# Last super-block: the new key and value rows of three head pairs by block transposes and a DRAM way, the last two projection jobs over 512 columns, and the last row tile scaled on two engines

## The chip, the cores and the metric

One core of one Trainium2 chip. The metric is device time in microseconds (us) of one execution. The kernel before takes 1251.13 us, the median of three runs (1250.59 to 1251.42). The engines are called as in the profile: PE is TensorE (matrix products and PE transposes), PEld its weight loads, DVE is VectorE, ACT is ScalarE, POOL is GpSimd, and SP is the engine that issues nearly all DMAs.

## The reference

One layer of a streaming encoder on 2048 prompt rows and 64 sample rows of width 1024. RMSNorm, one input projection into 4096 features, two head groups side by side, an output projection, a residual and a last RMSNorm:

```python
aq, ak, av, ag, hq, hf, hi, hg = split(rms_norm(x, ln_g) @ w_in)      # 8 x 512 features
o_a = attention(aq, ak, av, rel_bias) * silu(ag)                      # 8 heads x 64, band of 576 keys
o_b, S = hgrn2(hq, hf, hi, hg, lb, norm_g, s0)                        # 4 heads x 128, gated recurrence
y = rms_norm(x + concat([o_a, o_b]) @ w_out, ln_f_g)
new_k, new_v = ak[-512:], av[-512:]                                   # rows x features
```

The outputs are y for prompt and sample, the last 512 rows of the keys and of the values (512 x 512 each), the recurrent states, and the same for the sample. All is float32; a product is made of three float32r products of high and low parts.

## The kernel before

The prompt is cut into four super-blocks of 512 rows (the second also carries the 64 sample rows). A super-block is a list of 32 projection jobs (`JOBS`), each one feature block of 128 features: `hf hq hi hg` for a recurrent head, `pg pq pk pv` for a pair of attention heads. Attention heads are handled as four pairs, 0 to 3. One job (`project`, L539) is 24 matmuls over 512 columns into one of two `acc` banks of PSUM: features lie on partitions, rows of the sequence on columns. When a job ends, an evacuation routine (`ev_q`, `ev_k`, `ev_v`, `ev_v_last`, `ev_g` and the like) takes the bank to SBUF.

Every engine's instruction order is made in advance by a planner (`Plan`) that keeps a model of engine times and of tokens: one token for each buffer of a kind. The tokens that matter here are `acc` (2 banks), `tr` (2 PSUM banks for PE transposes), `sig` (2 SBUF tiles of 128 x 512), `vT` (3 tiles of 128 x 512) and `w` (4 weight tiles). `silu_to` and `ev_f` need a `sig` tile to evacuate their bank. On the chip each engine works its list in order and waits on semaphores; SP does the same with its DMAs, so a DMA that waits holds up those behind it.

In the first three super-blocks values go through `ev_v` (L840): `turn_blocks` (L666) turns 32x32 blocks on DVE, and `turn_rows` (L677) finishes the transpose by four DMAs to a DRAM scratch (`way`) and one DMA back; then `split_rows` makes the two parts that attention needs. In the last super-block all four pairs use `ev_v_last` (L811) instead: ACT copies the bank to a `vT` tile, PE turns it in two groups of four 64x64 transposes (one for each head), and `new_rows` (L624) turns it again with four 128x128 PE transposes into a `tr` bank, from which DVE copies to a `sig` tile and one DMA writes the new value rows. `ev_k` (L790) calls `new_rows` for the new key rows in the same way: four 128x128 PE transposes, one DVE copy, one DMA. The order of the last jobs is changed by hand (L48): `... pv2 pq2 pk2 hi3 hg3 pg2 pv3 pq3 pk3 pg3`.

The last two jobs of each super-block are worked in halves of 256 columns, in the order job 31 first half, job 32 first half, job 31 second half, job 32 second half (L2004), so that the x tiles of the next super-block can be written into the first half while the second is still read.

After the jobs come the output steps: 14 steps of 12 matmuls of 512 columns for each of four 512-row blocks (seven products for 256 rows, a Strassen scheme), with a sample step between. They start while attention of pair 3 is still running, and need weight tiles that are loaded into rooms that the projections and attention leave. `out_norm` (L1823) ends each row tile: ACT squares and sums, then Ln and Exp give the scale, DVE multiplies by scale and gain, SP writes the rows. For the last two row tiles (`end`) this is done in two halves of 512 columns, one after the other.

Of the kernel before, what the change touches and what calls it, by code (L numbers as in the profile page):

```python
# [8 lines left out]
F32 = mybir.dt.float32  # L9
# [3 lines left out]
ALU = mybir.AluOpType  # L13
# [4 lines left out]
P = 128  # L18
D = 1024
# [4 lines left out]
NPAIR = 4  # L24
# [159 lines left out]
def hymba_step(  # L184
# [24 lines left out]
    act = nc.scalar  # L209
    dve = nc.vector  # L210
    pool = nc.gpsimd
    pe = nc.tensor
    sp = nc.sync
# [9 lines left out]
    C = Plan()  # L223
    uid = [0]

    def T(pool_, shape, dt, tag, **kw):
        uid[0] += 1
        return pool_.tile(list(shape), dt, tag=tag, name=f"{tag}_{uid[0]}", **kw)
# [389 lines left out]
    def rows_out(src, out, cols, t):  # L618

        rows = src.shape[0]  # L620
        sp.dma_start(out[:rows, cols].rearrange("p (a j) -> p a j", a=4), src.rearrange("p (a j) -> p a j", a=4))
        return C.dma(rows)

    def new_rows(src, off, bn, p, out_p, out_s, tok, t):  # L624
# [29 lines left out]
            tk["sig"].put()  # L654
        tk["tr"].put(1, t)

    def split_rows(src, v, h, t0, nt, rows, t):
        s = src.rearrange("p (h a t j) -> p h a t j", h=2, a=2, t=nt)[:, h]
        hi, lo = (v[:rows, h, t0 : t0 + nt, x, :].rearrange("p t (a j) -> p a t j", a=2) for x in (h, 1 - h))
        act.copy(hi, s)  # L660
        t = C.act(nt * 64 + 80, t)
        yield "D", t
        dve.tensor_sub(lo, s, f32(hi))
        return C.dve(nt * 64 + 30, t)

    def turn_blocks(dst, src, bn):  # L666


        full = bn // P * P
        if full:  # L670
            dve.transpose(dst[:, :full].rearrange("p (b t j) -> p t b j", b=4, j=32),
                          src[:, :full].rearrange("p (t b j) -> p t b j", b=4, j=32))
        if bn > full:
            dve.transpose(dst[:, full:bn], src[:, full:bn])
        return C.dve(bn + 60)
# [63 lines left out]
    def pair_jobs(sb, p):  # L739
        t0, n = SUPER[sb][:2]  # L740
        last = sb == len(SUPER) - 1
        smp = n > WIN
        d = Pair()
        d.sb, d.p = sb, p
# [45 lines left out]
        def ev_k(acc, off, bn, t):  # L790
            yield from tk["vT"].get()
            yield "A", t
            kn = T(wk, [P, 512], F32, "vT", bufs=VTB)
            act.copy(kn[:, :bn], acc)
            t = C.act(bn, t)
            tk["acc"].put(1, t)
            c = slice(512 + off, 512 + off + bn)
            for h in range(2):
                yield lambda: d.open[h]
                yield "A", t  # L800
                act.copy(d.kd[own[h], h, c], kn[own[h], :bn])
                t = C.act(bn, t)
                yield "D", t
                dve.tensor_sub(d.kd[own[1 - h], h, c], kn[own[h], :bn], f32(d.kd[own[h], h, c]))
                t = C.dve(1.2 * bn, t)
                d.k_n[h] += bn
                d.k_t[h] = max(d.k_t[h], t)
            yield from new_rows(kn, off, bn, p, nk_prompt if last else None, nk_sample, tk["vT"], t)
            yield from got_all(True)

        def ev_v_last(acc, off, bn, t):  # L811
# [28 lines left out]
        def ev_v(acc, off, bn, t):  # L840
            yield from tk["vT"].get()
            yield "D", t
            vt = T(wk, [P, 512], F32, "vT", bufs=VTB)
            t = turn_blocks(vt, acc, bn)
            tk["acc"].put(1, t)
            t = yield from turn_rows(vt, bn, t)
            full = bn // P * P
            parts = [p_ for p_ in ((0, full, P, None),
                                   (full, P if bn > full else 0, bn - full, nv_sample)) if p_[1]]
            for c, w, rows, out in parts:  # L850
                if out is not None:
                    rows_out(vt[:rows, c : c + w], out, slice(p * P, (p + 1) * P), t)
            for h in range(2):
                yield lambda: d.open[h]
                for c, w, rows, _ in parts:
                    yield "A", t
                    t = yield from split_rows(vt[:rows, c : c + w], d.v, h, 4 + (off + c) // P, w // P, rows, t)
                d.v_n[h] += bn
                d.v_t[h] = max(d.v_t[h], t + 500.0)
            tk["vT"].put(1, t)  # L860
            yield from got_all(False)

        def all_in():
# [37 lines left out]
            yield from gate(acc, off, bn, t)  # L901
            d.sg_n += bn

        return d, dict(g=ev_g, q=ev_q, k=ev_k, v=ev_v_last if last else ev_v)

    def softmax_rows(d, h, qc, spans, bcol, nk, out):

# [915 lines left out]
    def out_norm(o, tile_, half, t):  # L1823

        rows = o["rows"]
        x = o["res"][tile_]
        end = o is outp.get(len(pairs) - 1)
        yield "A", t
        yield from tk["ck"].get()
        junk = T(wk, [P, D], mybir.dt.bfloat16, "ck", bufs=1)  # L1830
        ss = T(wk, [P, 1], F32, "ss", bufs=4)
        act.activation(junk[:rows, :512], x[half][:rows], AF.Square, accum_out=ss[:rows])  # L1832
        t = C.act(800, t)
        tk["ck"].put()
        if tile_ not in o["first"]:
            o["first"].add(tile_)
            b0 = T(wk, [P, 1], F32, "b0", bufs=4)
            yield "D", t
            dve.tensor_scalar(b0[:rows], ss[:rows], 1.0 / D, EPS, ALU.mult, ALU.add)
            C.dve(10, t)  # L1840
            o["b0"][tile_] = b0
            return
        yield lambda: tile_ in o["b0"]
        r = T(wk, [P, 1], F32, "rstd", bufs=4)
        act.activation(r[:rows], ss[:rows], AF.Ln, bias=o["b0"][tile_][:rows], scale=1.0 / D)
        act.activation(r[:rows], r[:rows], AF.Exp, scale=-0.5)
        t = C.act(400, t)
        y = o["y"][tile_]
        if x[3] is not None and not end:
            yield "D", t  # L1850
            dve.scalar_tensor_tensor(x[3][:rows], x[3][:rows], r[:rows], g_in[:rows], ALU.mult, ALU.mult)
            t = C.dve(1070, t)
            yield t
            sp.dma_start(y, x[3][:rows])
            C.dma(512 * rows / P)
        else:
            for a in range(2):
                c = slice(a * 512, a * 512 + 512)
                yield "D", t
                dve.scalar_tensor_tensor(x[a][:rows], x[a][:rows], r[:rows], g_in[:rows, c], ALU.mult, ALU.mult)  # L1860
                t = C.dve(530, t)
                yield t
                sp.dma_start(y[:, c], x[a][:rows])
                C.dma(256 * rows / P)
        for tag in x[2]:
            tk[tag].put(1, C.now + 4000.0)
# [46 lines left out]
    def program():  # L1913
# [65 lines left out]
        j = 0  # L1979
        for sb in range(nsb):  # L1980
            last = sb == nsb - 1
            halves = SUPER[sb][3]
            blocks = SUPER[sb][2]
            if sb == 2:
                C.spawn(out_weights(), 3)
            made = {}
            for u, (kind, g) in enumerate(JOBS[sb]):
                if u == len(JOBS[sb]) - 8:
                    if last:
                        C.spawn(out_load(0), 1.5)  # L1990
                        C.spawn(out_load(1), 1.6)
                        for rows in (out_rows_w(), out_rows_g(), out_rows_x(), out_rows_a()):
                            C.spawn(rows, 2)
                    else:
                        for half in range(2):
                            off, bn = SUPER[sb + 1][3][half]
                            for c in range(off, off + bn, P):
                                C.spawn(x_tile(sb + 1, half, c), 0.5 + 0.1 * half)
                if (kind[0], g) not in made:
                    d, evs = made[kind[0], g] = (head_jobs if kind[0] == "h" else pair_jobs)(sb, g)  # L2000
                    C.spawn((recurrence if kind[0] == "h" else attention)(d), 1)
                evac = made[kind[0], g][1][kind[1]]

                if u in (1, len(JOBS[sb]) - 1):  # L2004
                    for half in range(2):
                        yield from project(j - 1, [halves[half]], before, half == 1,
                                           lambda part, k0: x_ready(sb, half, part, k0))
                        yield from project(j, [halves[half]], evac, half == 1,
                                           lambda part, k0: x_ready(sb, half, part, k0))
                        if u > 1:  # L2010
                            x_left[sb, half] = True
                elif u not in (0, len(JOBS[sb]) - 2):
                    yield from project(j, blocks, evac)
                before = evac
                j += 1
        for i, k in steps:
# [147 lines left out]
```

## Time and profile before

| what | us |
|---|---|
| median of three runs | 1251.13 |
| profiled execution, own time | 1251.06 |
| its span, first to last instruction | 1249.3 |
| PE busy in the span | 1237.7 |
| DVE busy | 886.6 |
| ACT busy | 684.4 |
| POOL busy | 412.3 |
| last super-block, about (from the timeline) | 804 to 1065 |
| last matmul ends | 1242.7 |

Busy time is the union of an engine's instructions; matmuls overlap in a pipeline, so the distance from one start to the next says more than a matmul's own length. In a row of the timeline the first number is the start in us from the span's start, the second the time the merged instructions cover, then engine, line, operation, output<-inputs, shape and count, and in brackets the idle time before and what ended it. The profiled execution took 1.8 us more than its span.

### The profile page before, as it was taken

How to read it: one execution, taken by the hardware profiler on the slowest of the kernel's cores; microseconds unless marked ns; L12 is line 12 of the kernel's file. 1: busy time of each engine (PE TensorE's matmuls, PEld its weight loads, DVE VectorE, ACT ScalarE, POOL GpSimd, SP SyncE). 2: the span in 40 equal slices, each digit the busy share in tenths (PEclk: the TensorE clock that was granted, in tenths of full speed). 3: DMA queues.
4: the chain of work that ended last, by engine and by line, in shares of the span. 5: the costliest groups of instructions: out<-in, count | busy, mean ns of one | idle time of the engine just before them, and what ended most of it. 6: DMA issues, size and time to landing. Idle time of an engine off the chain costs nothing. (4 is left out here: it accounts for less than half of the span.)

```text
span 1249.3 us, 21363 instructions
## 1 busy us (share of the span) xinstructions
PE 1237.7 (99%) x7520; PEld 1088.6 (87%) x7520; DVE 886.6 (71%) x1889; ACT 684.4 (55%) x1534; POOL 412.3 (33%) x702
## 2 busy tenths in 40 slices
PE   9999999999999999999999999999999999999997
PEld 8888888999999999998888888988888888788786
DVE  7697878866767578776576677775757476767775
ACT  6354545665656556574555566664655445643443
POOL 7666564101020111200233242133241103474543
PEclk9999999999999999999999999999999999999999
DMA  8897888666565474654777778687766655887431
GB/s 337 301 325 257 313 301 318 203 192 222 166 195 166 144 276 155 206 178 150 284 247 252 266 263 280 227 258 248 231 243 210 218 203 211 333 273 237 139 123 68
DMA packets 137956, 287.94 MB, mean 230 GB/s; under 512 B 35257, under 2 KB 79289, under 8 KB 120186
## 3 DMA queue, kind: packets, MB, share of 16 engines
q1 hardware_dynamic: 137560, 286.58, 67.6%
q8 instruction: 59, 0.97, 0.3%
q14 instruction: 47, 0.39, 0.1%
q10 hardware_dynamic: 290, 0.01, 0.0%
HBM read 195.31 MB, written 92.27 MB: 230 GB/s over the span
## 5 line engine op out<-in xcount | busy, mean ns | idle before, releaser
L249 PE MATMUL acc<-xh,w 128*128 128x512 f32 (+2 forms) x2752 | 568.6, 345 | 0.5 <-ACT xh L409 0.5
L249 PEld LDWEIGHTS acc<-xh,w 128*128 128x128 f32 x2752 | 439.3, 189 | 50.6 <-ACT xh L409 0.9
L249 PE MATMUL acc<-xl,w 128*128 128x512 f32 (+2 forms) x1376 | 294.8, 345 | 0.0
L249 PEld LDWEIGHTS acc<-xl,w 128*128 128x128 f32 x1376 | 221.1, 189 | 24.4
L939 ACT ACTIVATE pr<-pr,nm 128x640 f32<-128x640 f32 (+4 forms) x132 | 100.4, 761 | 60.0 <-DVE nm L922 59.5
L951 ACT CAST ph<-tr 128x512 fp32r<-128x512 f32 (+3 forms) x176 | 88.2, 507 | 78.5 <-PE pv L249 45.8
L922 DVE CUSTOM_DVE_ANT_0 pr<-s,bias 128x640 f32<-128x640 f32 (+4 forms) x128 | 94.2, 736 | 41.1 <-PE s L249 40.3
L473 POOL TENSOR_TENSOR w<-wraw,w 128x256 fp32r<-128x256 f32 x120 | 102.4, 884 | 55.0 <-DVE w L468 43.1
L954 DVE TENSOR_TENSOR ph<-tr,ph 128x512 fp32r<-128x512 f32 (+3 forms) x176 | 101.2, 588 | 26.3 <-ACT ph L951 25.5
L249 PE MATMUL pv<-ph,v 128*128 128x256 f32 (+2 forms) x344 | 98.6, 370 | 0.1
L253 PE MATMUL tr<-ident,pr 128*128 128x128 f32 x580 | 88.1, 273 | 1.3 <-DVE ph L954 1.3
L993 DVE TENSOR_TENSOR mixa<-mixa,pv 64x256 f32<-64x256 f32 (+1 forms) x144 | 56.9, 395 | 43.3 <-ACT mixa L989 39.7
L510 POOL TENSOR_TENSOR xn<-wraw,xn 128x256 fp32r<-128x256 f32 x48 | 39.0, 814 | 142.4 <-ACT xn L507 137.1
L1095 POOL TENSOR_TENSOR mixa<-mixa,sga 128x256 f32<-128x256 f32 (+1 forms) x36 | 27.9, 776 | 162.8 <-DVE mixa L993 152.0
L253 PEld LDWEIGHTS tr<-ident,pr 128*128 128x128 f32 x580 | 69.7, 140 | 10.9 <-issue 1.7
L943 DVE TENSOR_SCALAR pr<-pr,sm 128x640 f32<-128x640 f32 (+4 forms) x132 | 74.6, 565 | 4.7
L1532 POOL TENSOR_TENSOR k<-ob 128x512 f32<-128x512 f32 (+2 forms) x20 | 18.2, 910 | 176.0 <-ACT ob L1523 136.0
L575 ACT ACTIVATE sig<-acc 128x512 f32<-128x512 f32 (+2 forms) x64 | 32.2, 503 | 74.6 <-PE acc L249 72.0
L249 PEld LDWEIGHTS pv<-ph,v 128*128 128x128 f32 (+1 forms) x344 | 58.2, 189 | 7.3 <-issue 0.5
L989 ACT COPY mixa<-pv 64x256 f32<-64x256 f32 (+1 forms) x72 | 25.2, 350 | 64.8 <-PE pv L249 59.5
L249 PE MATMUL s<-kd,q 128*128 128x320 f32 (+2 forms) x232 | 55.8, 310 | 0.0
L249 PE MATMUL s<-kd,ql 128*128 128x320 f32 (+2 forms) x232 | 55.5, 309 | 0.0
(333 smaller groups left out, 2133.3 us busy)
## 6 DMA issues: line engine op xcount, KB each, us to landing
w<-wd SPq DMA_DIRECT2D x96, 1024.0 KB, 5.8
wd<-w SPq DMA_DIRECT2D x32, 1024.0 KB, 7.3
wraw<-in_w_in_dram SPq DMA_DIRECT2D x30, 512.0 KB, 5.3
wod<-xn SPq DMA_DIRECT2D x28, 512.0 KB, 5.5
xn<-in_x_prompt_dram SPq DMA_DIRECT2D x23, 512.0 KB, 4.6
bias<-biasd SPq DMA_DIRECT2D x24, 320.0 KB, 5.9
carry<-kd SPq DMA_DIRECT2D x12, 512.0 KB, 7.0
carry<-v SPq DMA_DIRECT2D x12, 512.0 KB, 5.5
```

Of the source, the lines that this page charges most:

```text
L249: pe.matmul(out, w, x, **kw)
L253: pe.transpose(out, x, idn)
L473: pool.tensor_sub(w[:, 1, k : k + 2], raw[:, k : k + 2], f32(w[:, 0, k : k + 2]))
L510: pool.tensor_sub(f32r(st[:, c.start + 512 : c.stop + 512]), src[:, c], st[:, c])
L575: act.activation(sig[:, :bn], acc, AF.Exp, scale=-1.0)
L922: dve.tensor_tensor_reduce(s[:, :nk].rearrange("p (a c) -> p a c", a=ns), sps[:, :ns, :kn], d.bias[:, h, bcol : bcol + nk].rearrange("p (a ...
L939: act.activation(s[:, :nk], s[:, :nk], AF.Exp, bias=nm[:, 0:1], scale=-1.0, accum_out=sm)
L943: dve.tensor_scalar(s[:, :nk], s[:, :nk], sm, None, ALU.mult)
L951: act.copy(ph[:krows, 0, :wid], pt[:krows, :wid])
L954: dve.tensor_sub(ph[:krows, 1, :wid], pt[:krows, :wid], f32(ph[:krows, 0, :wid]))
L993: dve.tensor_add(mix[hs, :qn], mix[hs, :qn], pv[hs, i, :qn])
L1095: pool.tensor_mul(mix[:, :n], mix[:, :n], d.sg[:, g0 : g0 + n])
```

## The change

Four things are changed.

1. In the last super-block, pairs 0 to 2 use `ev_v` for the values like the earlier super-blocks, and write the new value rows from the turned tile by `rows_to`, four DMAs of 64 KB. The `vT` token comes back 4 us later.
2. For the same pairs the new key rows go by `block_rows`: a `sig` tile, 32x32 block transposes on DVE, the DRAM way, and four DMAs of 64 KB. The `sig` token comes back 4 us after the last of them is planned.
3. In the last super-block the last two jobs run over 512 columns, one after the other.
4. In the last row tile the half that is ready first is multiplied by the gain on DVE before its scale is known; at the end ACT multiplies this half by the scale and issues its DMA, while DVE does the other half as before.

```diff
+    def rows_to(src, out, off, w, p):
+        s4 = src.rearrange("q (a t j) -> q t a j", a=4, j=32)
+        for i in range(w // P):
+            row = off + i * P
+            sp.dma_start(out[row : row + P, p * P : (p + 1) * P].rearrange("q (a j) -> q a j", a=4), s4[:, i])
+            C.dma(64)
+            yield C.now + 800.0
+
+    def block_rows(src, off, bn, p, out, tok, t):
+        yield from tk["sig"].get()
+        yield "D", t
+        st = T(wk, [P, 512], F32, "sig", bufs=2)
+        t = turn_blocks(st, src, bn)
+        tok.put(1, t)
+        t = yield from turn_rows(st, bn, t)
+        yield t
+        yield from rows_to(st[:, :bn], out, off, bn, p)
+        tk["sig"].put(1, C.now + 4000.0)
...
+        by_blocks = last and p < NPAIR - 1
...
-            yield from new_rows(kn, off, bn, p, nk_prompt if last else None, nk_sample, tk["vT"], t)
+            if by_blocks:
+                yield from block_rows(kn, off, bn, p, nk_prompt, tk["vT"], t)
+            else:
+                yield from new_rows(kn, off, bn, p, nk_prompt if last else None, nk_sample, tk["vT"], t)
...
+                elif by_blocks:
+                    C.spawn(rows_to(vt[:, c : c + w], nv_prompt, off + c, w, p), 2)
...
-            tk["vT"].put(1, t)
+            tk["vT"].put(1, t + (4000.0 if by_blocks else 0.0))
...
-        return d, dict(g=ev_g, q=ev_q, k=ev_k, v=ev_v_last if last else ev_v)
+        return d, dict(g=ev_g, q=ev_q, k=ev_k, v=ev_v_last if last and not by_blocks else ev_v)
...
+            if end and tile_:
+                yield "D", 0.0
+                c = slice(half * 512, half * 512 + 512)
+                dve.tensor_mul(x[half], x[half], g_in[:, c])
+                C.dve(530)
+                o["scaled"] = half
             return
...
+        elif end and tile_:
+            a = o["scaled"]
+            act.mul(x[a], x[a], r)
+            act.dma_start(y[:, a * 512 : a * 512 + 512], x[a])
+            c = slice((1 - a) * 512, (1 - a) * 512 + 512)
+            dve.scalar_tensor_tensor(x[1 - a], x[1 - a], r, g_in[:, c], ALU.mult, ALU.mult)
+            sp.dma_start(y[:, c], x[1 - a])
...
-                if u in (1, len(JOBS[sb]) - 1):
+                if u == 1 or (u == len(JOBS[sb]) - 1 and not last):
...
-                elif u not in (0, len(JOBS[sb]) - 2):
+                elif u != 0 and (last or u != len(JOBS[sb]) - 2):
                     yield from project(j, blocks, evac)
+                    if u == len(JOBS[sb]) - 1:
+                        x_left[sb, 0] = x_left[sb, 1] = True
```

## The prediction

> **What bounds the kernel now.** I read the page's engine table first, then the busy time by stretches, then PE's timeline in the last super-block, then the end.
>
> ```profile
> span 1249.3 us, 21363 instructions
> ## 1 busy us (share of the span) xinstructions
> PE 1237.7 (99%) x7520; PEld 1088.6 (87%) x7520; DVE 886.6 (71%) x1889; ACT 684.4 (55%) x1534; POOL 412.3 (33%) x702
> ```
>
> ```profile
> 540.00:804.00 264.00, 264.00 (x1575) 230.12 (x1575) 183.30 (x385) 154.01 (x329) 66.58 (x114) 1.00 0.71 242
> 804.00:1065.00 261.00, 261.00 (x1546) 224.34 (x1545) 174.30 (x359) 145.75 (x303) 69.53 (x123) 1.00 0.68 230
> 1065.00:1100.00 35.00, 33.38 (x177) 27.57 (x176) 26.28 (x58) 20.57 (x45) 19.08 (x24) 1.00 0.86 326
> 1100.00:1242.50 142.50, 141.21 (x618) 114.29 (x616) 99.73 (x150) 60.33 (x151) 75.64 (x89) 1.00 0.52 163
> ```
>
> The columns of the second view are the stretch, its length, then busy time (and count) of PE, PEld, DVE, ACT, POOL, the granted clock, the DMA share and GB/s. In the stretch of the last super-block (804 to 1065) PE is never idle and the clock is granted in full. It idles 1.62 us in the hand-over to the output steps and 1.29 us after. So PE's own list sets the time, and work taken off that list comes out of the span unless a new wait takes its place. As overlapping matmuls can make a busy row look full, I go by starts:
>
> ```profile
> 991.87 0.61 PE L249 MATMUL acc<-xl,w 128*128 128x512 f32 x2
> 992.42 0.46 PE L253 MATMUL tr<-ident,vT 64*128 64x64 f32 x4
> 992.80 1.67 PE L249 MATMUL acc<-xl,w 128*128 128x512 f32 x6
> 994.31 1.09 PE L249 MATMUL acc<-xh,w 128*128 128x512 f32 x4
> 995.34 0.46 PE L253 MATMUL tr<-ident,vT 64*128 64x64 f32 x4
> 995.73 2.58 PE L249 MATMUL acc<-xh,w 128*128 128x512 f32 x10
> 998.14 0.60 PE L253 MATMUL tr<-ident,vT 128*128 128x128 f32 x4
> 998.50 0.72 PE L249 MATMUL acc<-xh,w 128*128 128x512 f32 x2
> 999.05 2.01 PE L249 MATMUL acc<-xl,w 128*128 128x512 f32 x8
> 1000.90 3.79 PE L249 MATMUL acc<-xh,w 128*128 128x512 f32 x16
> ...
> 1009.67 0.60 PE L253 MATMUL tr<-ident,vT 128*128 128x128 f32 x4
> 1010.02 0.71 PE L249 MATMUL acc<-xh,w 128*128 128x512 f32 x2
> 1010.57 0.46 PE L249 MATMUL s<-kd,q 128*128 128x320 f32 x2
> ```
>
> Matmuls of 512 columns with nothing between them start every 0.231 us (8 from 999.05 to 1000.90). The rows above are the value path of pair 2: two groups of four small transposes, one group of four full ones.
>
> **Part 1 and 2: transposes leave PE.** From 991.87 to 999.05 are 7.18 us and 24 matmuls; 24 x 0.231 = 5.54 us, so the three groups cost 1.64 us with the change of shape before and after them. The key group (1009.67): 0.90 us to 1010.57 less 2 x 0.231 is 0.44 us. A pair pays 2.08 us, three pairs **6.24 us**. Pair 3 keeps its transposes. I take pairs 0 and 1 as pair 2, whose rows are shown; all three have the same counts.
>
> On transposes a rule of the Trainium skill (VectorE: DVE Perf Modes, The three transpose paths) gives 390 ns for a 128x128 transpose on TensorE. By that figure 48 transposes would be 18.7 us, an estimate. The rows disagree: four full ones take 0.36 us start to start, so I stay with the rows.
>
> What replaces them lies on DVE, SP and the DMA queues:
>
> ```profile
> L671 DVE STREAM_TRANSPOSE vT<-acc 128x512 f32<-128x512 f32 x18 | 12.8, 711 | 5.3 <-PE acc L249 5.2
> ```
>
> ```profile
> way<-vT SPq DMA_DIRECT2D x72, 64.0 KB, 5.0
> vT<-way SPq DMA_DIRECT2D x18, 256.0 KB, 5.6
> ...
> out_dram<-sig SPq DMA_DIRECT2D x7, 256.0 KB, 5.8
> ...
> out_dram<-vT SPq DMA_DIRECT2D x4, 32.0 KB, 1.8
> ```
>
> Per pair DVE gets two block transposes of 0.71 us and loses two copies of 512 columns out of PSUM; ACT loses one copy. DVE is busy 174 of 261 us there, so I cost this at nothing; without that cover it would be 3 x 2 x 0.71 = 4.3 us at most. SP gets 16 more DMAs a pair (four to the way, one back and four of rows in place of one, for keys and for values). It issues, it does not compute. Behind these stand the weight loads, which have four buffers, so about three jobs (3 x 24 x 0.231 = 16.6 us) until a late one is felt.
>
> Two waits are added. Attention's values of pairs 0 to 2 now come over the way, 0.7 + 5.0 + 5.6 us and the issues, some 13 us after the job. PE is covered by the next projection jobs. This wait exists already in the super-block before (540 to 804), which uses the same path, and PE idles 0.00 us in it; I cost it at nothing, and as bound at one landing of 5.6 us. And each key block holds one of the two `sig` tiles for 0.7 + 5.0 + 5.6 + 5.8 us and the issues, 17 to 21 us. Behind it wait the Exp of the next `hf`, `hq` or `hg` evacuation on ACT, behind that the other work of ACT, and PE when no `acc` bank is free. One tile is left, and one evacuation at a time needs it, so I take nothing here; the price if it isn't so is the third rival.
>
> **Part 3: 512 columns.**
>
> ```profile
> 1060.89 2.08 PE L249 MATMUL acc<-xh,w 128*128 128x256 f32 x16
> 1062.81 1.12 PE L249 MATMUL acc<-xl,w 128*128 128x256 f32 x8
> 1063.77 1.12 PE L249 MATMUL acc<-xh,w 128*128 128x256 f32 x8
> ```
>
> At 256 columns a start comes every 0.120 us (24 from 1060.89 to 1063.77, 2.88 us). Two jobs in halves are 96 of them, 11.52 us; over 512 columns 48 x 0.231 = 11.09 us. That is **0.43 us**. A page of the Trainium skill (TensorE: Matmul & The Clock Gate, Back-to-back issue gap) puts the gap of an isolated matmul at N / 2.4 + 2.5 ns; by it the two would be 10.48 and 10.36 us, an estimate, and this part worth 0.12 us. The trace's starts at 512 columns are 15 ns above that figure and at 256 columns 11 ns, so I keep 0.43.
>
> The order changes too: the key job of pair 3 is done after half of the last two jobs, not after three quarters, but its first 256 columns after half, not a quarter. Attention of pair 3 then begins about 11.09 / 2 - 11.52 / 4 = 2.7 us later and has all its keys 11.52 x 3/4 - 5.55 = 3.1 us earlier. I take these as cancelling, and the idle 1.62 us of the hand-over as staying.
>
> **Part 4: the end.**
>
> ```profile
> 1242.76 0.69 DVE L1783 TENSOR_TENSOR pr<-pr,acc 128x512 f32<-128x512 f32 x1 [2.05 <-issue]
> ...
> 1244.56 0.20 ACT L1846 ACTIVATE rstd<-rstd 128x1 f32<-128x1 f32 x1
> 1244.80 1.41 DVE L1860 SCALAR_TENSOR_TENSOR pr<-pr,rstd,gin 128x512 f32<-128x512 f32 x2
> 1245.61 0.96 SPq L1863 DMA_DIRECT2D out_dram<-pr  x2
> ```
>
> ```profile
> L1279 ACT COPY gi<-vT 128x512 f32<-128x512 f32 x12 | 7.4, 616 | 5.1 <-DMA vT<-way 5.1
> ```
>
> ```profile
> 0.83 0.52 ACTq L1921 DMA_DIRECT2D gin<-in_ln_in_g_dram  x1
> ```
>
> Now DVE scales both halves in 1.41 us, and SP issues the last DMA as the second of two in 0.96 us, ending at 1246.57. After the change DVE scales one half, to 1244.80 + 0.75 = 1245.55 (a little over half of 1.41, as the two overlap), and SP issues one DMA of about 0.33 us from 1245.61 to 1245.94. ACT's multiply is not in the trace; the nearest row is its copy of the same size, 0.62 us: 1244.76 + 0.62 = 1245.38, and its DMA issue of 0.52 us (the only place where ACT issues) ends at 1245.9. So **0.63 us** are saved; bounds are 0.7, one DVE half, and a loss of 0.3 if ACT's issue takes twice as long as at the start. The added multiply by the gain, some 0.7 us, falls into DVE's idle 2.05 us before 1242.76.
>
> **The sum.** 6.24 + 0.43 + 0.63 = 7.30 us. Against the profiled execution's 1251.06 us that is 1243.76; the median of the runs shown is 0.07 us above that execution, so 1243.8 us. Nothing else in the output steps changes: their PE work is the same, only earlier.
>
> **The rivals.**
>
> *The hand-over gives a part back.* PE already stops there once:
>
> ```profile
> 1084.19 0.41 PE L253 MATMUL tr<-ident,pr 128*128 128x128 f32 x2 [1.35 <-DVE ph L954]
> ```
>
> Here PE's transposes waited for DVE, which waited for ACT, whose list had waited for loads. All this is placed by a planner, and a change of 7 us in front of it places it anew. If attention of pair 3, 2.7 us later, is followed as late by the weights that are loaded into its rooms, or if another such stop of 1.35 us comes in, 1.4 to 4.8 us are given back: 1245.2 to 1248.6 us. For it: the DMA share is 0.86 in this stretch. Against it: the full keys are there earlier. The same stop can as well go: then 1242.4 us, and with the rest of the 1.62 us 1242.2.
>
> *The way is late and PE waits.* If the values of each of the three pairs come one landing (5.6 us) too late for PE and half of that is felt, 8.4 us are lost and 7.3 won: 1252 us; a little less felt gives no change, 1249 to 1253. For it: DMA share 0.68. Against it: the super-block before with the same path and no idle.
>
> *Slower: the key block keeps its `sig` tile too long.* It decides when the hold of 17 to 21 us goes beyond the time until two evacuations want a tile at once. After a key job come pv, hf and hq: 16.6 us of bare projections, and with attention between them (261 us for 32 jobs, 8.2 us each) 24.5 us; then a bank more of cover, 5.5 us. The rows go out in pieces of 128 bytes. If each 64 KB took what 256 KB take now, 5.8 us, one behind the other, the hold would be 12 + 23 = 35 us, 5 us beyond 24.5 + 5.5, for three pairs 15 us against 7.3: 1259 us. The row against it: the sample's value rows, in the same 128-byte pieces, land in 1.8 us for 32 KB. The Trainium skill (DMA: Bandwidth & Descriptors, Specifications) has a rule against this change: below 512 bytes a transfer is not at line rate, with a read-modify-write. By that rule this rival would stand; the 1.8 us row speaks against its size here.
>
> **How the numbers follow.** PE full and nothing given back, 1241 to 1245 us: 0.60. Hand-over gives back, 1245 to 1248.6: 0.22. No change, by a late way: 0.10. Slower by the key block or by several waits: 0.08. A difference under 0.2% (2.5 us) is about what a measurement of this kernel can't tell from no change. So faster 0.82, same 0.10, slower 0.08. The range goes from 1240.8 (all 1.62 us of the hand-over's idle and the 1.29 us after it gone) to 1248.6, the end of the second case.
>
> **What would show it.** Right: 48 fewer `tr<-ident,vT` matmuls and 48 fewer matmuls of `acc` in PE's count, 7424 in all; the last super-block about 6.7 us shorter with PE idle near 0; the hand-over's idle near 1.6 us; the last DMA issued about 3.3 us after the last matmul, not 3.9. Wrong: PE idle before `acc` or `pv` in the last super-block with a releaser of ACT `sig` (the key block), of ACT or DVE `v` behind `vT<-way` (the late way), or new idle between the last projection and the first steps on `kd` weights (the hand-over).

## The result, and the profile after

The changed kernel takes **1260.47 us** (median of four runs, 1259.39 to 1261.39) against 1251.19 us of the kernel before beside it: ratio 1.0078, 95% interval 1.0065 to 1.0090. The forecast was 1243.8 us, with 1248.6 as the top of the range. The profiled execution took 1261.39 us.

The head of the page, then the busy time by stretches (columns as in the prediction):

```profile
span 1259.7 us, 21223 instructions
## 1 busy us (share of the span) xinstructions
PE 1234.2 (98%) x7424; PEld 1083.7 (86%) x7424; DVE 887.3 (70%) x1885; ACT 681.1 (54%) x1526; POOL 413.2 (33%) x702
```

```profile
804.00:1059.00 255.00, 254.29 (x1447) 216.99 (x1446) 171.33 (x350) 140.09 (x290) 69.93 (x122) 1.00 0.77 247
1059.00:1065.00 6.00, 4.80 (x25) 3.68 (x23) 3.07 (x8) 1.12 (x3) 1.76 (x3) 1.00 0.50 160
1065.00:1100.00 35.00, 23.69 (x116) 19.93 (x117) 20.16 (x45) 16.99 (x37) 10.20 (x13) 0.80 0.65 244
1100.00:1251.50 151.50, 149.31 (x658) 120.70 (x656) 105.92 (x162) 64.61 (x161) 83.30 (x98) 1.00 0.52 167
```

PE has the 96 matmuls less that were foreseen (7424), and until 1059 it idles only 0.71 us: the super-block is shorter, as forecast. The loss is in the next 41 us: 11.31 us of PE idle between 1065 and 1100, and a granted clock of 0.80. PE's longest wait, with the line waited at, the releaser, and us in total, times, longest:

```profile
PE acc L249 <- DVE sga L580: 12.4, 1, 12.4
```

One stop of 12.4 us is more than the whole loss. The timeline around it:

```profile
1058.57 1.28 DVE L645 COPY sig<-tr 128x512 f32<-128x512 f32 x2
...
1059.28 0.39 SPq L650 DMA_DIRECT2D out_dram<-sig  x1
...
1059.44 0.62 PE L249 MATMUL acc<-b11h,slot 128*128 128x512 f32 x2
...
1061.65 0.37 SPq L1667 DMA_DIRECT2D sig<-mixd  x1
...
1062.66 0.86 SPq L2064 DMA_DIRECT2D w<-wod  x2
...
1063.61 0.69 SPq L650 DMA_DIRECT2D out_dram<-sig  x1
1073.45 0.60 ACT L575 ACTIVATE sig<-acc 128x512 f32<-128x512 f32 x1 [13.33 <-DMA out_dram<-sig]
...
1075.56 0.69 DVE L580 TENSOR_TENSOR sga<-acc,sig 128x512 f32<-128x512 f32 x1 [13.20 <-ACT sig L577]
...
1076.31 2.08 PE L249 MATMUL acc<-w,slot 128*128 128x512 f32 x4 [12.40 <-DVE sga L580]
```

Read from below: PE has no free `acc` bank, because the last projection job, the gate of pair 3, is still in one. Its silu on ACT needs a `sig` tile. Both tiles were filled with pair 3's value and key rows at 1058.57. The first tile came free with its row DMA, but was taken at 1061.65 by a load of the *second output block* (`sig<-mixd`). The second tile's rows were ready at 1058.57 + 1.28 = 1059.85, but their DMA stood on SP's list behind that load, the load of the last norm's gain (512 KB) and 2 MB of weights, was issued at 1063.61, and freed ACT 9.8 us later. The same place in the kernel before:

```profile
1057.24 0.38 ACT L575 ACTIVATE sig<-acc 128x256 f32<-128x256 f32 x1 [0.34 <-PE acc L249]
...
1060.40 1.01 DVE L645 COPY sig<-tr 128x512 f32<-128x512 f32 x2
...
1061.11 0.94 SPq L650 DMA_DIRECT2D out_dram<-sig  x2
...
1065.32 0.63 PE L249 MATMUL acc<-b11h,slot 128*128 128x512 f32 x2
...
1067.20 0.39 ACT L575 ACTIVATE sig<-acc 128x256 f32<-128x256 f32 x1 [1.89 <-DMA out_dram<-sig]
...
1069.88 5.51 SPq L1642 DMA_DIRECT2D sig<-mixd  x2
```

There the gate's first half is out of its bank before the rows come, the second half waits 1.89 us, and the loads of the second block take the tiles only after it. What lets these loads go is `all_in`, inside `pair_jobs`: "projected" is set when the values, keys and queries of pair 3 are counted in. Neither the key rows' tile nor the gate is asked for. The last two jobs are pair 3's keys and gate. In halves, the gate was half evacuated and half a job from its end when the keys were complete; over 512 columns the keys are complete a whole job (24 x 0.231 = 5.5 us) before it.

The stop brings a second loss. The windows around it:

```profile
1064.00:1076.30 12.30, 0.00 (x0) 0.00 (x0) 0.69 (x1) 2.79 (x6) 0.00 (x0) 0.64 0.62 227
1076.30:1078.30 2.00, 1.99 (x5) 1.50 (x6) 1.43 (x4) 1.25 (x3) 0.00 (x0) 0.50 0.36 108
1078.30:1080.00 1.70, 1.70 (x10) 1.70 (x9) 1.45 (x5) 0.72 (x2) 0.00 (x0) 0.50 0.97 294
1080.00:1082.00 2.00, 2.00 (x8) 1.62 (x8) 1.84 (x4) 1.15 (x3) 0.00 (x0) 0.73 0.95 338
```

After the stop the clock is granted at 0.50, and at 0.73 in the fourth stretch: 3.70 x 0.50 + 2.00 x 0.27 = 2.4 us more, an estimate, as PE is busy in nearly all of it. If the clock is either 1 or 0.5, the 0.64 of the 12.30 us of idle say that it fell after 0.28 x 12.30 = 3.4 us. The Trainium skill (TensorE: Matmul & The Clock Gate, Part 1: The HAM clock gate) has the clock halved after an idle window of about 3.4 us and back after as much busy time. The trace agrees with the first; the return took 1076.31 to about 1081.1, 4.8 us (the 0.73 again split into 1 and 0.5).

So by steps, after less before: the first output step starts at 1059.44 for 1065.32, -5.9 us; from there to the end of the last matmul it is 192.2 us (to 1251.60) for 177.3 (to 1242.67), +14.8 us; from the last matmul to the end of the span 8.1 us for 6.6, +1.5 us. Sum +10.4, the difference of the spans. Of the 14.8 us, 11.8 are idle time (PE idles 14.7 us there, 12.4 of them in the stop, for 2.9 before) and 2.4 the clock by the estimate; 0.6 us are left without a row.

### The profile page after: what moved, and what is told of

Read it like the earlier page. It is cut to its first block, busy times and chain, and to the rows that moved or that the text cites. A ratio compares the mean times of both kernels' runs of the same rounds, so it can differ in the third digit from the quotient of the medians.

```text
span 1259.7 us, 21223 instructions
## 1 busy us (share of the span) xinstructions
PE 1234.2 (98%) x7424; PEld 1083.7 (86%) x7424; DVE 887.3 (70%) x1885; ACT 681.1 (54%) x1526; POOL 413.2 (33%) x702
## 4 chain that ended last, share of the span: by engine, by line
PE 92%; DVE 2%; DMA 2%; POOL 1%; issue 1%; ACT 1%; DVEq 0%; SPq 0%; POOLq 0%; ACTq 0%
PE acc L249 66%; PE g L249 8%; PE tr L253 6%; PE pv L249 6%; PE s L249 6%; PE g L253 1%; DMA out_dram<-sig 1%; DMA w<-wod 1%; DMA vT<-way 0%; POOL sig L1738 0%; POOL xn L1813 0%; DVE slot L1720 0%; POOL bias L1813 0%; POOL vT L1738 0%; PE tr L249 0%
```

## The experiments

Each is made from the changed kernel. The kernel before, run beside them on the same chip, took 1250.74, 1250.33 and 1250.17 us in the three groups; each ratio is to its own group.

**The parts by themselves.** No part 3 is the two conditions of the job loop as before; no part 1 and 2, and no part 4:

```diff
-        by_blocks = last and p < NPAIR - 1
+        by_blocks = False
...
-            if end and tile_:
+            if False:
...
-        elif end and tile_:
+        elif False:
```

Parts 1 and 2 alone:

> Parts 1 and 2 alone (value and key rows of pairs 0 to 2 by block transposes and the DRAM way; last two jobs in halves and last row tile as before). Theory A, the 12.4 us stop of PE comes from part 3 (512-column jobs let the loads of the output step take the first free sig tile, and the last silu gets the tile whose row DMA stands behind the weight loads): the stop is absent, 6.2 us of transposes leave PE, about 1245 us (1243 to 1247). Theory B, the stop comes from the new way moving the schedule: PE waits about 12 us for DVE sga here too, about 1257 us or more.

Measured 1245.59 us, ratio 0.9959 (0.9944 to 0.9974). The transposes' gain is there, 5.1 us by the ratio. In the profiled execution, the slowest of the four (1246.88 us), part of it is given back at a new small stop:

```profile
1013.30 4.04 SPq L710 DMA_DIRECT2D way<-vT  x4
...
1018.71 0.32 SPq L714 DMA_DIRECT2D vT<-way  x1
...
1025.67 0.62 ACT L1304 COPY gi<-vT 128x512 f32<-128x512 f32 x1 [6.13 <-DMA vT<-way]
1026.19 0.58 ACT L976 CAST ph<-tr 128x512 fp32r<-128x512 f32 x1
1026.80 0.69 DVE L979 TENSOR_TENSOR ph<-tr,ph 128x512 fp32r<-128x512 f32 x1 [4.01 <-ACT ph L976]
...
1027.55 0.74 PE L249 MATMUL pv<-ph,v 128*128 128x512 f32 x2 [1.77 <-DVE ph L979]
```

The recurrent job hi3 has used the way all along. Its way now shares SP's list with the key rows' way; ACT waits 6.13 us for it with attention's cast queued behind, and PE stops for 1.77 us. In the kernel before ACT did not wait for this copy. That is the prediction's late way, on a job that it didn't name; that the shared list makes it late is argued from the order of the rows, not tested. The size differs from trace to trace: in the changed kernel PE stops 0.7 us at this place, in the kernel of parts 1, 2 and 4 in halves (below) 0.2 us.

Part 3 alone:

> Part 3 alone (last two jobs over 512 columns; all pairs keep their PE transposes; last row tile as before). Theory A: the stop before the second output step comes in without parts 1 and 2, PE idle of about 12 us with releaser DVE sga behind ACT sig behind a row DMA, and some 2 us at half clock after it: about 1251.2 - 0.4 + 14 = 1265 us (1260 to 1267). Theory B: no stop, 1250 to 1252 us.

Measured 1271.39 us, ratio 1.0160 (1.0142 to 1.0178). Part 3 by itself carries the loss, and more of it. But the form isn't the stop expected. PE's waits and SP's list:

```profile
PE acc L249 <- DMA ph<-wod: 5.8, 1, 5.8
PE pv L249 <- DVE ph L979: 3.9, 2, 3.8
```

```profile
1063.05 0.39 SPq L650 DMA_DIRECT2D out_dram<-sig  x1
1063.49 2.36 SPq L1667 DMA_DIRECT2D sig<-mixd  x2
...
1113.97 0.38 SPq L650 DMA_DIRECT2D out_dram<-sig  x1
```

Here the second block's loads took *both* tiles; the rows that were not yet out were sent 50.5 us after those loads, and attention of pair 3 and the weights that go into its rooms (`ph<-wod`) were late too. Between the first output step and the last matmul the kernel takes 20.4 us more than before; PE's idle time grows by 14.1 us, and the clock is granted at 0.95 on average for 1.00. The expectation missed both the path and the total: 1271.39 us lie 6 us above its 1265 and outside its range. That it is the same shortage of tiles is shown by the hold below, which takes this loss away.

Part 4 alone:

> Part 4 alone (last row tile by ACT and DVE). PE's list is that of the kernel before. Theory A, the planner now puts the second half of the row tile before the last one behind the last tile's half on DVE, and its DMA is issued last: last matmul to end of span 8.1 us as in the changed kernel, against 6.6 before, so 1251.2 + 1.5 = 1252.7 us. Theory B, the prediction's: 0.6 us faster, 1250.6 us.

Measured 1251.85 us, ratio 1.0009 (1.0000 to 1.0019): no gain, at most a small loss. Why is seen at the end of the changed kernel, which part 4 alone repeats (8.0 us from the last matmul to the end of the span there, 8.1 here):

```profile
1252.29 0.74 DVE L1898 SCALAR_TENSOR_TENSOR bias<-bias,rstd,gin 128x512 f32<-128x512 f32 x1
...
1253.72 0.75 DVE L1892 SCALAR_TENSOR_TENSOR pr<-pr,rstd,gin 128x512 f32<-128x512 f32 x1 [0.69 <-ACT rstd L1877]
1254.39 0.75 DVE L1898 SCALAR_TENSOR_TENSOR bias<-bias,rstd,gin 128x512 f32<-128x512 f32 x1
...
1254.54 0.33 SPq L1893 DMA_DIRECT2D out_dram<-pr  x1
1254.97 1.27 SPq L1901 DMA_DIRECT2D out_dram<-bias  x2
```

`bias` is the tile *before* the last. Its two halves were done together at 1243.36 in the kernel before; now DVE does one, idles 0.69 us for the last tile's scale, does the last tile, and then the other half. The last DMA's issue ends at 1256.24, 4.6 us after the last matmul, not the 3.3 forecast.

**Is it the taken tile?** The changed kernel whole, with the loads of the second block held until the gate is evacuated (called the hold from here on):

```diff
-            if last and p == NPAIR - 1 and d.v_n[1] == d.k_n[1] == d.q_n[1] == n:
+            if last and p == NPAIR - 1 and d.v_n[1] == d.k_n[1] == d.q_n[1] == d.sg_n == n:
...
             d.sg_n += bn
+            all_in()
```

> The changed kernel, except that the loads of the second output block may begin only when the gate of pair 3 is evacuated too, so the last silu takes the sig tile whose row DMA was issued first (landed within 2.5 us in the changed kernel). Theory A: the 12.4 us wait and the half clock behind it go, 1260.5 - 14.5 = 1246 us; the loads behind the second row DMA may still be late for the third product's weights, up to 5 us of that come back: 1246 to 1251 us. Theory B, the tile is not the cause: PE still waits about 12 us at the same place, 1258 us or more.

Measured 1249.13 us, ratio 0.9986 (0.9977 to 0.9996): 11.5 us less than the changed kernel by the two ratios (0.0092 x 1251). Its timeline:

```profile
1058.46 0.39 SPq L650 DMA_DIRECT2D out_dram<-sig  x1
1059.49 0.89 SPq L2065 DMA_DIRECT2D w<-wod  x2
1060.47 0.55 SPq L650 DMA_DIRECT2D out_dram<-sig  x1
1061.11 0.60 ACT L575 ACTIVATE sig<-acc 128x512 f32<-128x512 f32 x1 [2.32 <-DMA out_dram<-sig]
...
1063.97 0.73 PE L249 MATMUL acc<-w,slot 128*128 128x512 f32 x2 [1.48 <-DVE sga L580]
```

The gate's silu now gets the first tile that comes free, and PE's stop is 1.48 us for 12.40. That the order of the tiles lets the long stop come is shown by this. The second row DMA still stands behind the weights here (1060.47); the next user of its tile, a load, begins only at 1069.71, 9.2 us later, but PE does not wait for that one.

**Or the place of the row DMA on SP's list?** The weights of the third product only after pair 3's key rows are on the list:

```diff
             if last and p == NPAIR - 1 and d.v_n[1] == d.k_n[1] == d.q_n[1] == n:
                 have.add("projected")
...
+            if last and k and p == NPAIR - 1:
+                have.add("rows3")
...
+            if k == 2:
+                yield lambda: "rows3" in have
```

> The changed kernel, except that the third product's weights are loaded only after the key rows of pair 3 are on SP's list, so the row DMA that the last silu waits for no longer stands behind 2 MB. Theory A2 (the wait is long because of that place: 4 us on the list and 9.7 us to landing): the row DMA goes out near 1062 us, lands in 2.5 to 4 us, PE waits 3 to 5 us instead of 12.4, no half clock to speak of: 1250 to 1254 us. If the taken tile alone sets it: PE waits 10 us or more, 1258 us or more.

Measured 1255.61 us, ratio 1.0046 (1.0031 to 1.0061). PE's longest wait and the timeline:

```profile
PE acc L249 <- DVE sga L580: 6.8, 1, 6.8
```

```profile
1060.68 0.37 SPq L1669 DMA_DIRECT2D sig<-mixd  x1
1061.69 0.38 SPq L650 DMA_DIRECT2D out_dram<-sig  x1
1062.17 0.99 SPq L2066 DMA_DIRECT2D w<-wod  x2
1066.86 0.60 ACT L575 ACTIVATE sig<-acc 128x512 f32<-128x512 f32 x1 [7.71 <-DMA out_dram<-sig]
```

Ahead of the weights the row DMA is issued at 1061.69 and frees ACT 5.2 us later, in place of 1063.61 and 9.8 us; PE's stop is 6.8 us. So, by one trace of each kernel, the place on the list behind the weights makes 5.6 of the 12.4 us, and the taken tile most of the rest (1.5 us stay with the hold): a result between the two expectations. That a DMA lands late behind others of the same list goes with the Trainium skill (DMA: Bandwidth & Descriptors, Two DMAs through the same engine are not ordered): within one queue of one DMA engine, descriptors start in order.

**What is part 3 worth without the stop?** Part 3 alone with the same hold:

> Part 3 alone, with the loads of the second output block held until the gate of pair 3 is evacuated. In the run of part 3 alone the row DMA of pair 3's keys came 51 us after the other one, because those loads had taken both sig tiles, and the key rows kept a transpose bank meanwhile. Theory A (both stops have this one root, the early taking of sig tiles): the 20 us go, 1250 us (1249 to 1253). Theory C (part 3 is slow of itself, as attention of pair 3 begins later): 1260 us or more.

Measured 1251.79 us, ratio 1.0011 (1.0001 to 1.0020). The waits of 5.8 and 3.8 us that part 3 alone had are gone, and so is the loss but for 1.4 us (0.1 to 2.5). The 0.43 us of gain aren't there: the first output step starts at 1065.45, for 1065.32 before.

**Part 4 mended, and the values of pair 3 too.** Both without part 3; the tile before the last is scaled and sent without the planner's stop between its halves. In the second kernel pair 3's values take the way as well:

```diff
             for a in range(2):
                 c = slice(a * 512, a * 512 + 512)
-                yield "D", t
+                if not end or not a:
+                    yield "D", t
...
-                yield t
+                if not end:
+                    yield t
```

> Parts 1, 2 and 4 (last two jobs in halves), and the row tile before the last one has its two halves scaled and sent without a stop for the planner between them. If part 4 lost only because its second half came after the last tile: last matmul to end of span 6.1 us, against 6.7 with parts 1 and 2 alone and 8.1 in the changed kernel, so 1245.6 - 0.6 = 1245.0 us (1244 to 1246.5). If ACT's own DMA or multiply is what costs: 7.5 us or more there, 1246.5 us or more.

> The same, and the values of pair 3 by the DRAM way too (its key rows stay with PE): 12 more transposes leave PE. If PE's list sets the time here too, 1.6 us less than the run before, 1243.4 us (1242 to 1245). If the later values of pair 3 hold up attention and with it the output weights, or their tile is missing to the loads of the output: slower than that run by 2 us or more.

Measured 1245.72 us, ratio 0.9962 (0.9948 to 0.9977), and 1246.26 us, ratio 0.9963 (0.9949 to 0.9978). The first has the forecast order at its end and is no faster than parts 1 and 2 alone. The second takes twelve more transposes from PE and gains nothing: its profiled execution, the slowest of five, has new waits of PE behind DVE, 2.2 and 1.1 us at `pv` and 1.4 us at `s`. The forecast for it was missed by nearly 3 us.

**All four parts, mended, and the same without part 3:**

> All four parts, the second output block's loads held until pair 3's gate is evacuated, and the tile before the last scaled and sent without a stop for the planner. Theory A (after the 12.4 us stop, what is left of the loss is the order of the halves at the end, 8.05 us from the last matmul to the end in place of 6.7): the held kernel's 1249.1 us less 1.4 = 1247.7 us. Theory B (the end is set by the last DMAs and the order on DVE costs nothing of itself): 1249.1 us again. If part 3 were worth its 0.43 us once mended, the kernel would have to come under the 1245.7 us of parts 1, 2 and 4 in halves: neither theory expects that.

> Parts 1 and 2, last jobs in halves, the same hold and the same mended end: the kernel above without part 3. It differs from the kernel of parts 1, 2 and 4 in halves (1245.7 us) by the hold alone, and from the kernel above by part 3 alone. Theory A (the hold costs nothing where no gate stands behind those loads): 1245.7 us, within 1. Rival (the loads of the second output block come later and the output steps wait for them): 1247 us or more, and then the 2 us that the held kernel lies above are the hold's and not part 3's.

Measured 1247.34 us (1246.0 to 1248.68), ratio 0.9976 (0.9966 to 0.9986), and 1245.58 us (1244.71 to 1246.64), ratio 0.9963 (0.9950 to 0.9977). The mended end gives back 1.3 us of the held kernel's time by the ratios and 1.8 by the medians, about the 1.4 expected. The hold costs nothing where part 3 is left out. With part 3 the kernel is 1.8 us slower by the medians, though the two intervals overlap. In the profiled executions, which are only 0.4 us apart, only the kernel with part 3 has a wait of 1.5 us for `acc` behind DVE `sga`.

The end of the first of the two:

```profile
1238.25 1.41 DVE L1900 SCALAR_TENSOR_TENSOR bias<-bias,rstd,gin 128x512 f32<-128x512 f32 x2
...
1239.69 0.72 ACT L1890 ACTIVATE pr<-pr,rstd 128x512 f32<-128x512 f32 x1
...
1240.44 0.37 ACTq L1891 DMA_DIRECT2D out_dram<-pr  x1
1240.50 0.33 SPq L1894 DMA_DIRECT2D out_dram<-pr  x1
```

The last issue ends at 1240.83, 3.3 us after the last matmul (1237.56), as predicted for part 4. Yet the span ends at 1244.3, 6.7 us after that matmul, and before it was 6.6. The 0.6 us won at the issue are lost between issue and end: 3.5 us in place of 1246.57 to 1249.3, 2.7 us (3.4 us in the kernel of parts 1, 2 and 4 in halves, with and without the hold). The two last DMAs now start within 0.1 us of each other; whether that makes them land later, I haven't tried.

No kernel tried beats parts 1 and 2 alone, with or without the mended end: 1245.6 us, 0.4% under the kernel before.

## Why the prediction was wrong

*PE bounds the super-block, and transposes cost PE time:* right. PE's count, the idle near 0 and the first output step 5.9 us earlier are as said (6.7 forecast for the super-block).

*Part 1 and 2, 6.24 us:* right in mechanism. By itself it measured 5.1 us; the interval (0.0026 to 0.0056, so 3.3 to 7.0 us) holds 6.24. A stop at hi3's way, 0.2 to 1.8 us by the trace, was costed at nothing: I asked whether the *new* users of the way would be late, and not whether an old user behind them would. The rival of the key block with its `sig` tile did not come: between 804 and 1059 PE idles 0.71 us. The row DMAs in the page's table (form, count, KB each, us from issue to landing):

```profile
out_dram<-vT SPq DMA_DIRECT2D x12, 64.0 KB, 3.9
out_dram<-sig SPq DMA_DIRECT2D x12, 64.0 KB, 2.1
```

The 64 KB in 128-byte pieces took 2.1 and 3.9 us in the median and not the 5.8 that the rival needed.

*Part 3:* the step that failed. It reads "I take these as cancelling, and the idle 1.62 us of the hand-over as staying". I had weighed when pair 3's attention gets its keys, and not what else the order of the halves had held apart: the gate's first half evacuated before the rows need the tiles, and "projected" set late. With both gone, two tiles had more claimants than they could serve at one moment: two sets of rows, the gate and the next block's loads. That is the tile of my third rival with another holder, at the place of my first, and neither price (15 us there by a slow DMA, 1.4 to 4.8 here) was worked out from it. The runs put this part at +20.0 us alone (0.0160 x 1251), +1.4 us alone with the hold (0.0011 x 1251), and +1.8 us in the mended whole. So even without the big stop the 0.43 us did not come; alone with the hold the sign is the other one, in the whole the intervals overlap. In the whole a row for it is PE's wait of 1.5 us: the gate's 512 columns are evacuated as one, behind a row DMA. Alone with the hold the silu waits only 0.18 us for its tile, and where the time goes there stays open.

*Part 4, -0.63 us:* the step "DVE scales one half, to 1244.80 + 0.75" took DVE's list as it was. The planner put the second half of the tile before last behind it, +1.5 us at the end. And where the order was as forecast, the end still did not move: the sum counted to the last issue and took the landing behind it as fixed, 2.7 us, which became 3.5. ACT's multiply (0.72 us) and issue (0.37) were near their estimates (0.62, 0.52).

*The chances:* slower had 0.08 and no mechanism of the hand-over in it; the hand-over's rival ended at 1248.6. What was missed was one look at the conditions by which the next stage is let go, beside the tokens that it takes.

## What to carry to other kernels

When work in halves is merged, list what each half released (a bank, a tile, a condition for the next stage) and ask who now stands in between: the matmuls saved are the small number. Where a buffer kind is shared by two stages, let the next stage take it only when the last user of the stage before has had it; one such condition was worth 11.5 us here, and cost nothing in the kernel that did not need it. A saving at the last DMA's issue counts only if its landing comes earlier too.

## What was not expected of the hardware

A row DMA of 256 KB that stood on SP's list behind loads of 256 KB, 512 KB (the gain) and two of 1 MB freed its waiter 9.8 us after its issue began; behind the first two alone it took 5.2 us, and ahead of all of them 2.6 us or less (issue at 1058.46, ACT released at 1061.11). The place on the list is not all: in the kernel before the first row DMA (1061.11) landed after 6.0 us, though SP had issued nothing for 3.8 us; the DMA share was 1.00 from 1057 to 1061, and 0.75 in the 4.4 us ahead of the one that took 2.6 us. And a stop of 12.4 us costs PE 14.8: the half clock behind it is 2.4 us more.
